# Taking the low part of every third feed-forward weight piece from an accumulating DMA instead of VectorE

## The chip, the cores and the metric

The kernel runs on one core of a Trainium2 chip. The metric is device time in microseconds (us), from a run without a profile; next to it stands one profiled execution, whose trace is read here. A core has five engines with a queue each: TensorE (PE; its weight loads are PEld), VectorE (DVE), ScalarE (ACT), GpSimd (POOL) and SyncE (SP). DMAs are issued from SP, ACT or POOL and run on the core's 16 DMA engines.

## The reference, cut to what matters

Two transformer-like blocks follow each other on 256 tokens of width 2048: first a block of gated linear recurrences, then one of windowed attention and gated linear attention, with a feed forward at its end. Only that end is touched:

```python
mixed = jnp.concatenate([attn_out, gla_out], axis=-1) @ w_out[l]        # (256,2048) @ (2048,2048)
x = x + mixed
h = rmsnorm(x, ffn_norm_w[l])
x = x + (jax.nn.silu(h @ w_gate[l]) * (h @ w_up[l])) @ w_down[l]        # hidden width 5632
return rmsnorm(x, final_norm_w)
```

All operands are float32.

## The kernel before

Every weight matrix is read once from DRAM and multiplied in a split form: a number is the sum of a high part (rounded to the matmul's float32r format) and a low part (what the rounding left). For each block of 128 input rows and each half of the tokens three matmuls are made: activation high by weight high (`wh`), activation high by weight low (`wl`), activation low by weight high, all into one PSUM bank. This is `products`, line 185.

The work is cut into **chunks** (a weight block of 16 or 22 row blocks by 512 columns, a few narrower) and each chunk into **pieces** of at most 1536 columns per partition: with 512 columns a piece holds 2 or 3 row blocks. A 16-block chunk has pieces of 2, 3, 3, 2, 3, 3 blocks, a 22-block chunk (the down matrix) 2, 3, 3, 3, 2, 3, 3, 3. A piece of n blocks is 6n matmuls, 12 or 18. There are 588 pieces in 98 chunks.

`run_stream` goes through the pieces in order. At piece i it issues `load(i+3)` (line 246: one DMA on SP into a `wr` buffer) and `cut(i+2)`: ScalarE casts `wr` into `wh` (line 259), VectorE subtracts `wh` from `wr` into `wl` (line 260). `wr`, `wh` and `wl` have three buffers each, so piece i takes the buffer of piece i-3, and its cast can't start before TensorE has read the last of piece i-3. Between the pieces, side generators put the other work of the block (transposes at line 203, the gate's tanh at line 182, `ff_up` at lines 1354 and 1355). The order of the instructions on each engine isn't that of the code alone: a scheduler in the framework puts them in the order in which, by its own costs, they become ready.

The feed forward has two halves of 2816 hidden columns. In each half come six gate chunks alternating with six up chunks (five of 512 columns and one of 256), then four down chunks. Before it stand the four chunks of the output projection (`mix_out`).

Of the kernel before, what the change touches and what calls it, by code (L numbers as in the profile page):

```python
# [11 lines left out]
F32 = mybir.dt.float32  # L12
F32R = mybir.dt.float32r
AF = mybir.ActivationFunctionType
ALU = mybir.AluOpType
# [4 lines left out]
P = 128  # L20
# [69 lines left out]
class Chunk:  # L90


    def __init__(self, src, width, nk, opnd, done, k0=0, kind="tok", tag="mm"):
        self.src, self.width, self.nk, self.opnd, self.done, self.k0 = src, width, nk, opnd, done, k0

        self.kind, self.tag = kind, tag
        self.per = max(1, min(nk, WN // width))
        self.po = None


class Opnd:
# [22 lines left out]
def kernel(ctx, tc, a, out, dbg=None):  # L124
    nc = tc.nc
    PE, V, A, G, SP = nc.tensor, nc.vector, nc.scalar, nc.gpsimd, nc.sync
# [14 lines left out]
    def nm(s):  # L141
        uid[0] += 1
        return f"{s}{uid[0]}"
# [16 lines left out]
    def v3(t, b):  # L160
        return t.rearrange("p (a b) -> p a b", b=b)
# [19 lines left out]
    def act(o, x, f, **kw):  # L181
        return A.activation(out=o, in_=x, func=f, **kw)  # L182
# [36 lines left out]
    chunks = []  # L219
# [31 lines left out]
    def cut(i):  # L251
        if i >= len(pieces) or i in split:
            return
        ch, k, n = pieces[i]
        w = raw.pop(i)
        sz = n * ch.width
        h = wp.tile([P, WN], F32R, tag="wh", name=nm("wh"), bufs=3)
        l = wp.tile([P, WN], F32R, tag="wl", name=nm("wl"), bufs=3)
        A.copy(out=h[:, :sz], in_=w[:, :sz])  # L259
        V.tensor_tensor(out=l[:, :sz], in0=w[:, :sz], in1=h[:, :sz].bitcast(F32), op=ALU.subtract)  # L260
        split[i] = (v3(h[:, :sz], ch.width), v3(l[:, :sz], ch.width))

    sides = deque()
# [1217 lines left out]
    for hf in range(2):  # L1481
        off = 0
        while off < HALF:
            w = min(512, HALF - off)
            c0 = hf * HALF + off
            add(Chunk([wg[:, c0:c0 + w]], w, 16, op3, lambda po, c0=c0, w=w: ff_gate(po, c0, w)))
            add(Chunk([wu[:, c0:c0 + w]], w, 16, op3, lambda po, c0=c0, hf=hf, w=w: ff_up(po, c0, w, hf, c0 // P)))
            off += w
        for n in range(4):
            add(Chunk([wd[:, n * 512:(n + 1) * 512]], 512, HALF // P, opf[hf],  # L1490
                      lambda po, n=n, hf=hf: ff_down(po, n, hf), k0=hf * HALF // P))
    startup()
    run_stream()

# [22 lines left out]
```

## Time and profile before

| | us |
|---|---|
| median of the two timed runs (2348.87 and 2351.42) | 2350.14 |
| the profiled execution's own time | 2350.77 |
| its span, first to last instruction | 2349.0 |
| TensorE busy in the span | 2330.5 |
| VectorE busy | 1384.8 |
| ScalarE busy | 1062.6 |
| GpSimd busy | 91.1 |

The profiled execution lies 0.6 us above the median, and 1.8 us of it are outside the span. Busy times are sums over the span; those of TensorE overlap the pipelined ends of its matmuls. The feed forward and the two chunks ahead of it take about the last 690 us.

### The profile page before, as it was taken

Reading aid. Unit: us, or ns where it says so; the run is one execution under the profiler, and the core shown is the slowest. Engines: PE = TensorE matmul, PEld = TensorE weight load, DVE = VectorE, ACT = ScalarE, POOL = GpSimd, SP = SyncE. Lnnn points to the kernel's source line nnn. Section 1 sums busy time; section 2 is a strip of 40 time slices with the busy share of each in tenths; the row PEclk is TensorE's granted clock in tenths of the full one; section 3 lists DMA queues with packets and bytes.
Section 4 is the critical chain, followed back from the end, with each engine's and each line's share of the span. In section 5 each row is a group of like instructions: output and inputs, shape, how many; then the busy total and the mean of one; then the engine's idle time right before and its main releaser. Section 6 shows DMA issues by size and latency. Waiting matters only on the chain.

```text
span 2349.0 us, 28535 instructions
## 1 busy us (share of the span) xinstructions
PE 2330.5 (99%) x11392; PEld 1930.0 (82%) x11392; DVE 1384.8 (59%) x1689; ACT 1062.6 (45%) x1240; POOL 91.1 (4%) x122
## 2 busy tenths in 40 slices
PE   8999999999999999999999999999999999999998
PEld 6888888888888888888887877888888888888886
DVE  6778677686576555455555566655545544555554
ACT  5554444544454444444444465444444333434443
POOL 0101001000000000000000000000000000000000
PEclk9999999999999999999999999999999999999999
DMA  6656545665555556566565544556655555665554
GB/s 207 188 177 202 180 142 157 188 196 188 169 159 163 180 188 210 184 200 210 180 219 179 157 141 130 166 180 201 188 192 186 191 191 187 192 194 187 188 197 152
DMA packets 226340, 427.89 MB, mean 182 GB/s; under 512 B 17256, under 2 KB 25872, under 8 KB 226208
## 3 DMA queue, kind: packets, MB, share of 16 engines
q1 hardware_dynamic: 220288, 411.07, 54.7%
q0 software_dynamic: 5056, 13.70, 2.1%
q8 instruction: 89, 1.46, 0.2%
q10 hardware_dynamic: 864, 1.31, 0.2%
q14 instruction: 43, 0.35, 0.0%
HBM read 422.31 MB, written 3.73 MB: 181 GB/s over the span
## 4 chain that ended last, share of the span: by engine, by line
PE 98%; DMA 1%; ACT 0%; issue 0%; DVE 0%; SPq 0%; POOLq 0%; POOL 0%; ACTq 0%; DVEq 0%
PE mm L185 91%; PE sp L185 4%; PE sp L203 3%; PE sp L699 1%; PE sp L1129 0%; DMA wr<-in_w_in_dram 0%; DMA pg<-in_x_dram 0%; ACT pg L182 0%; DVE wl L260 0%; ACT wh L259 0%; ACT hl L182 0%; SPq L246 0%; DVE pg L179 0%; ACT hp L182 0%; POOLq L1513 0%
## 5 line engine op out<-in xcount | busy, mean ns | idle before, releaser
L185 PE MATMUL mm<-wh,hl 128*128 128x512 f32 (+1 forms) x4864 | 1500.1, 387 | 1.6 <-ACT wh L259 1.6
L260 DVE TENSOR_TENSOR wl<-wr,wh 128x1536 fp32r<-128x1536 f32 (+3 forms) x588 | 919.3, 1567 | 751.6 <-ACT wh L259 750.7
L259 ACT CAST wh<-wr 128x1536 fp32r<-128x1536 f32 (+3 forms) x588 | 780.4, 1328 | 994.7 <-PE mm L185 943.1
L185 PEld LDWEIGHTS mm<-wh,hl 128*128 128x128 f32 x4864 | 904.7, 188 | 183.2 <-issue 4.9
L185 PE MATMUL mm<-wl,hl 128*128 128x512 f32 (+1 forms) x2432 | 941.9, 387 | 1.3 <-DVE wl L260 1.3
L185 PEld LDWEIGHTS mm<-wl,hl 128*128 128x128 f32 x2432 | 458.0, 188 | 89.7 <-DVE wl L260 1.9
L185 PE MATMUL mm<-wh,pg 128*128 128x512 f32 x1472 | 456.0, 390 | 0.0
L185 PEld LDWEIGHTS mm<-wh,pg 128*128 128x128 f32 x1472 | 276.2, 188 | 57.0
L185 PE MATMUL mm<-wl,pg 128*128 128x512 f32 x736 | 287.4, 390 | 0.0
L185 PEld LDWEIGHTS mm<-wl,pg 128*128 128x128 f32 x736 | 138.2, 188 | 29.2 <-DVE wl L260 0.9
L203 PE MATMUL sp<-con,pg 128*128 128x128 f32 x555 | 88.3, 275 | 4.1 <-DMA pg<-in_consts_dram 4.0
L203 PEld LDWEIGHTS sp<-con,pg 128*128 128x128 f32 x555 | 68.9, 141 | 21.0 <-issue 6.0
L179 DVE SCALAR_TENSOR_TENSOR pg<-cv,vt,pg 128x255 f32<-128x255 f32 (+2 forms) x144 | 61.4, 478 | 7.6 <-ACT pg L182 7.5
L185 PE MATMUL sp<-pg,pg 128*128 128x128 f32 (+3 forms) x320 | 50.7, 316 | 0.0
L179 DVE SCALAR_TENSOR_TENSOR pg<-pg,mm 128x512 f32<-128x512 f32 (+1 forms) x60 | 39.9, 665 | 16.5 <-ACT pg L182 14.8
L185 PEld LDWEIGHTS sp<-pg,pg 128*128 128x128 f32 (+1 forms) x320 | 43.0, 190 | 6.1 <-issue 2.5
L182 ACT ACTIVATE pg<-mm,rh 128x512 f32<-128x512 f32 x40 | 27.2, 687 | 33.8 <-PE mm L185 33.8
L182 ACT ACTIVATE pg<-pg 128x512 f32<-128x512 f32 (+2 forms) x54 | 35.3, 676 | 12.1 <-DVE pg L792 4.9
L182 ACT ACTIVATE pg<-mm,rstd 128x512 f32<-128x512 f32 x36 | 24.4, 687 | 32.2 <-PE mm L185 32.2
L182 ACT ACTIVATE pg<-sp,vt 128x256 fp32r<-128x256 f32 (+1 forms) x48 | 21.5, 471 | 25.7 <-PE sp L203 14.4
L179 DVE SCALAR_TENSOR_TENSOR hl<-sp,vt,hl 128x256 fp32r<-128x256 f32 x48 | 21.7, 479 | 14.0 <-ACT hl L182 13.9
L182 ACT ACTIVATE hl<-sp,vt 128x256 fp32r<-128x256 f32 x48 | 21.2, 478 | 16.1 <-PE sp L203 10.9
(245 smaller groups left out, 871.2 us busy)
## 6 DMA issues: line engine op xcount, KB each, us to landing
wr<-in_w_in_dram SPq DMA_DIRECT2D x208, 768.0 KB, 4.5
wr<-in_w_in_dram SPq DMA_DIRECT2D x104, 512.0 KB, 4.6
wr<-in_w_out_dram SPq DMA_DIRECT2D x48, 768.0 KB, 4.5
wr<-in_w_down_dram SPq DMA_DIRECT2D x48, 768.0 KB, 4.4
wr<-in_w_gate_dram SPq DMA_DIRECT2D x42, 768.0 KB, 4.4
wr<-in_w_up_dram SPq DMA_DIRECT2D x42, 768.0 KB, 4.4
wr<-in_w_out_dram SPq DMA_DIRECT2D x24, 512.0 KB, 5.1
wr<-in_w_gate_dram SPq DMA_DIRECT2D x20, 512.0 KB, 4.8
```

Of the source, the lines that this page charges most:

```text
L179: return V.scalar_tensor_tensor(out=o, in0=x, scalar=s, in1=y, op0=op0, op1=op1)
L182: return A.activation(out=o, in_=x, func=f, **kw)
L185: PE.matmul(o, l, r, start=start, stop=stop)
L203: PE.transpose(o, x, ident[:n, :n])
L259: A.copy(out=h[:, :sz], in_=w[:, :sz])
L260: V.tensor_tensor(out=l[:, :sz], in0=w[:, :sz], in1=h[:, :sz].bitcast(F32), op=ALU.subtract)
L699: PE.matmul(o, l, r_, start=True, stop=True, tile_position=(row, col))
```

## The change

A chunk gets a flag `acc`, set on the last 34 chunks: the second half of the output projection and the whole feed forward. In them, each piece whose number is a multiple of three gets its low part in another way. ScalarE writes minus the high part into `wl` (an activation with scale -1, whose output is rounded to float32r as the cast's is); then GpSimd issues a DMA that reads the same weights from DRAM a second time and adds them onto `wl`. The subtract on VectorE is left out for these pieces. There are 69 of them: 60 with 3 blocks of 512 columns, 5 with 2 blocks, 4 in the chunks of 256 columns. As three buffers go round, they are always the same buffer of `wl`.

```diff
@@ class Chunk
+        self.acc = False
@@ cut
         A.copy(out=h[:, :sz], in_=w[:, :sz])
-        V.tensor_tensor(out=l[:, :sz], in0=w[:, :sz], in1=h[:, :sz].bitcast(F32), op=ALU.subtract)
+        if ch.acc and i % 3 == 0:
+
+            act(l[:, :sz], w[:, :sz], AF.Copy, scale=-1.0)
+            G.dma_start(out=v3(l[:, :sz], ch.width), accum_op=ALU.add,
+                        in_=ch.src[0][(ch.k0 + k) * P:(ch.k0 + k + n) * P, :].rearrange("(k p) n -> p k n", p=P))
+        else:
+            V.tensor_tensor(out=l[:, :sz], in0=w[:, :sz], in1=h[:, :sz].bitcast(F32), op=ALU.subtract)
@@ the end of the list of chunks
+    for ch in chunks[-34:]:
+        ch.acc = True
     startup()
     run_stream()
```

Line numbers of the changed kernel are one higher up to line 260 and seven higher behind it; the new activation goes through the helper at line 183, the new DMA is line 264.

Three places show the new order. On ScalarE, in an up chunk of the first half, `wl2055` is the low part of a piece of the new kind, `wh2054` its high part, `wr2050` its raw weights, and `pg2056` the gate's tanh. Before:

```order
L259 CAST wh2051_12884<-wr2047_12864 128x1024 [waits DMAHW6_49,DVE_49,PE_49]
L259 CAST wh2054_12908<-wr2050_12882 128x1536 [waits DMAHW7_49,DVE_49,PE_49]
L182 ACTIVATE pg2056_12930<-mm2035_12786,r3h_117 128x512 [waits PE_49]
L182 ACTIVATE pg2056_12930<-mm2036_12787,r3h_117 128x512 [waits PE_49]
L259 CAST wh2058_12937<-wr2053_12906 128x1536 [waits DMAHW0_49,DVE_49]
```

After:

```order
L260 CAST wh2051_12898<-wr2047_12878 128x1024 [waits DMAHW6_49,DVE_49,PE_49]
L183 ACTIVATE wl2055_12923<-wr2050_12896 128x1536 [waits DMASW3_49,DMAHW7_49,PE_49,Activation_49]
L260 CAST wh2054_12922<-wr2050_12896 128x1536 [waits PE_49,Activation_49]
L183 ACTIVATE pg2056_12945<-mm2035_12799,r3h_117 128x512 [waits PE_49]
L183 ACTIVATE pg2056_12945<-mm2036_12800,r3h_117 128x512 [waits PE_49]
L260 CAST wh2058_12952<-wr2053_12920 128x1536 [waits DMAHW0_49,DVE_49]
```

The minus-high activation stands ahead of the cast of its own piece, and both ahead of the tanh, where one cast stood.

On TensorE, in the first gate chunk of the second half, `wh2313` and `wl2314` belong to a piece of the new kind, and `wh2316`, `wl2317` to the 2-block piece behind it. Before:

```order
L185 MATMUL mm2304_14659<-wh2313_14723,hl1878_11738 128x512 [waits Activation_49]
L185 MATMUL mm2305_14660<-wh2313_14723,hl1878_11738 128x512
L185 MATMUL mm2304_14659<-wl2314_14724,hl1878_11738 128x512 [waits DVE_49]
L185 MATMUL mm2304_14659<-wh2313_14723,hl1878_11738 128x512 x2
L185 MATMUL mm2304_14659<-wl2314_14724,hl1878_11738 128x512
```

After:

```order
L186 MATMUL mm2304_14697<-wh2313_14761,hl1878_11738 128x512 [waits Activation_49]
L186 MATMUL mm2305_14698<-wh2313_14761,hl1878_11738 128x512
L186 MATMUL mm2325_14838<-wh2316_14780,hl1878_11738 128x512 [waits Activation_49]
L186 MATMUL mm2326_14839<-wh2316_14780,hl1878_11738 128x512
L186 MATMUL mm2325_14838<-wl2317_14781,hl1878_11738 128x512 [waits DVE_49]
L186 MATMUL mm2325_14838<-wh2316_14780,hl1878_11738 128x512 x2
...
L186 MATMUL mm2304_14697<-wl2314_14762,hl1878_11738 128x512 [waits DMASW4_49]
```

All 12 matmuls of the 2-block piece now stand between the first two matmuls of the piece and its first `wl` matmul, which waits for the accumulating DMA. The order has this form at 13 of the 69 pieces, nearly all in the second half; at the piece of the new kind that comes next, only one 3-block piece is then left between it and the last piece of its kind.

On TensorE, in a gate chunk of the first half, `wl2076` is of the new kind, and `sp2084`, `sp2091` are transposes of the up chunk before. Before:

```order
L185 MATMUL mm2081_13078<-wh2075_13047,hl1878_11738 128x512
L185 MATMUL mm2080_13077<-wl2076_13048,hl1878_11738 128x512 [waits DVE_49]
L185 MATMUL mm2080_13077<-wh2075_13047,hl1878_11738 128x512 x2
L185 MATMUL mm2080_13077<-wl2076_13048,hl1878_11738 128x512
L185 MATMUL mm2080_13077<-wh2075_13047,hl1878_11738 128x512 x2
L203 MATMUL sp2084_13093<-con_84,pg2056_12930 128x128 [waits DVE_49]
```

After:

```order
L186 MATMUL mm2081_13095<-wh2075_13063,hl1878_11738 128x512
L204 MATMUL sp2084_13110<-con_84,pg2056_12945 128x128 [waits DVE_49]
L204 MATMUL sp2091_13157<-con_84,pg2056_12945 128x128 [waits PE_49]
L204 MATMUL sp2084_13110<-con_84,pg2056_12945 128x128 [waits DVE_49]
L204 MATMUL sp2084_13110<-con_84,pg2056_12945 128x128 x2
L204 MATMUL sp2091_13157<-con_84,pg2056_12945 128x128 x3
L186 MATMUL mm2080_13094<-wl2076_13064,hl1878_11738 128x512 [waits DMASW6_49]
```

Eight transposes have moved ahead of the first `wl` matmul; this is so at 7 pieces.

## Rows read from the trace of the kernel before

**Rows 1.** The page, its parts 1, 4 and 5: TensorE, the chain, two groups.

```profile
PE 2330.5 (99%) x11392; PEld 1930.0 (82%) x11392; DVE 1384.8 (59%) x1689; ACT 1062.6 (45%) x1240; POOL 91.1 (4%) x122
...
PE 98%; DMA 1%; ACT 0%; issue 0%; DVE 0%; SPq 0%; POOLq 0%; POOL 0%; ACTq 0%; DVEq 0%
...
L185 PE MATMUL mm<-wh,hl 128*128 128x512 f32 (+1 forms) x4864 | 1500.1, 387 | 1.6 <-ACT wh L259 1.6
...
L185 PE MATMUL mm<-wl,hl 128*128 128x512 f32 (+1 forms) x2432 | 941.9, 387 | 1.3 <-DVE wl L260 1.3
```

**Rows 2.** Two stretches of the feed forward: busy us by engine, clock, DMA share, GB/s.

```profile
1700.00:1836.00 136.00, 136.00 (x637) 113.43 (x636) 69.64 (x56) 56.62 (x50) 0.00 (x0) 1.00 0.59 188
...
1960.00:2200.00 240.00, 240.00 (x1094) 199.23 (x1093) 122.47 (x96) 98.38 (x85) 0.00 (x0) 1.00 0.60 190
```

**Rows 3.** Who waited for whom from 1640 us on: total, times, longest.

```profile
ACT wh L259 <- PE mm L185: 358.9, 169, 3.0
DVE wl L260 <- ACT wh L259: 316.4, 174, 3.3
```

**Rows 4.** Timeline of ScalarE: start, duration, what, idle before it.

```profile
1774.71 1.48 ACT L259 CAST wh<-wr 128x1536 fp32r<-128x1536 f32 x1 [2.60 <-PE mm L185]
1777.43 1.05 ACT L259 CAST wh<-wr 128x1024 fp32r<-128x1024 f32 x1 [1.24 <-PE mm L185]
1781.51 1.48 ACT L259 CAST wh<-wr 128x1536 fp32r<-128x1536 f32 x1 [3.02 <-PE mm L185]
...
1834.13 1.27 ACT L259 CAST wh<-wr 128x1280 fp32r<-128x1280 f32 x1
...
1838.15 1.26 ACT L259 CAST wh<-wr 128x1280 fp32r<-128x1280 f32 x1 [1.21 <-PE mm L185]
```

**Rows 5.** Timeline of TensorE around the same piece.

```profile
1774.06 0.39 PE L185 MATMUL mm<-wl,hl 128*128 128x512 f32 x1
...
1781.77 0.39 PE L185 MATMUL mm<-wl,hl 128*128 128x512 f32 x1
...
1782.45 0.39 PE L185 MATMUL mm<-wl,hl 128*128 128x512 f32 x1
```

**Rows 6.** Timeline of VectorE, the subtract of the same piece.

```profile
1776.23 1.76 DVE L260 TENSOR_TENSOR wl<-wr,wh 128x1536 fp32r<-128x1536 f32 x1 [2.32 <-ACT wh L259]
```

**Rows 7.** Groups by shape, whole span: count, busy us, mean ns, idle before.

```profile
L259 ACT CAST wh<-wr 128x1536 fp32r<-128x1536 f32 x388 | 574.2, 1480 | 773.5 <-PE mm L185 737.9 <-issue 22.3 <-DMA wr<-in_w_in_dram 11.9
...
L259 ACT CAST wh<-wr 128x1024 fp32r<-128x1024 f32 x184 | 193.6, 1052 | 209.7 <-PE mm L185 194.7 <-issue 9.1 <-ACT wh L259 3.5
...
L182 ACT ACTIVATE pg<-pg 128x1024 f32<-128x1024 f32 x14 | 14.8, 1058 | 5.0 <-DVE pg L792 4.9
```

**Rows 8.** Line 986, plain loads of 512 KB issued from GpSimd.

```profile
L986 POOL DMA_DIRECT2D pg<-in_x_dram x4: 727/744/755, 855.0 to 1097.7; - x4
...
DMA to landing us min/median/max: 4.1/4.4/5.2
```

**Rows 9.** Tile wr from 1700 us on: weight loads issued from SP.

```profile
L246 SPq DMA_DIRECT2D wr<-in_w_down_dram x64: 367/368/368, 1836.9 to 2319.0; - x64
...
DMA to landing us min/median/max: 3.6/4.4/6.4
```

**Rows 10.** Line 1374, loads of one DRAM row to all partitions, from GpSimd.

```profile
L1374 POOL DMA_DIRECT2D hp<-in_final_norm_w_dram x4: 536/539/604, 1611.9 to 2284.6; - x4
...
DMA to landing us min/median/max: 5.3/6.2/7.1
```

**Rows 11.** DMA from 1900 to 1922 us in 40 slices: busy tenths, GB/s.

```profile
DMA  9960001499985999526999300037973001399964
GB/s 287 335 250 34 0 0 37 93 335 376 410 205 93 354 384 410 194 63 156 372 357 354 127 0 0 0 48 197 324 268 115 0 0 11 82 313 384 398 268 104
```

**Rows 12.** Two stretches at the start, columns as in rows 2.

```profile
0.00:10.00 10.00, 5.98 (x32) 6.01 (x33) 0.76 (x3) 4.88 (x13) 1.79 (x7) 1.00 0.77 249
...
20.00:30.00 10.00, 7.07 (x31) 4.85 (x32) 5.73 (x13) 5.95 (x11) 0.00 (x0) 1.00 0.70 228
```

## The prediction

> **What bounds the kernel now.** I read the page first: TensorE is busy 99% of the span and makes 98% of the chain that ended last; before its `wh` and `wl` matmuls it idled 1.6 and 1.3 us in the whole run [rows 1]. The stretches of the feed forward say the same of the stage that is changed: TensorE 136.00 of 136.00 and 240.00 of 240.00 us, VectorE about half, ScalarE about four tenths, the DMA engines 0.59 and 0.60 of their time [rows 2]. The waits there show who follows whom: ScalarE's cast waits for TensorE (358.9 us in 169 waits), VectorE's subtract for the cast (316.4 us), and TensorE for neither [rows 3]. So VectorE's 69 subtracts, 1.76 us each [rows 6], lie beside other work. Taking them away can give back at most the 2.9 us of idling in rows 1. What is left to ask is whether the new path brings `wl` before TensorE wants it.
>
> **The window of a piece.** Rows 4 to 6 show one ordinary 3-block piece that would be of the new kind. The last `wl` matmul of the piece three before it, whose buffer it takes, starts at 1774.06 and ends at 1774.45. The cast starts at 1774.71; the 2-block piece is through 2.72 us later and the 3-block piece 4.08 us after that (next casts at 1777.43 and 1781.51), and the first `wl` matmul of the piece itself starts at 1781.77 [rows 4, 5]. A matmul takes a place of 0.227 us (three between 1781.77 and 1782.45). A handover costs 0.04 us: the cast ends at 1776.19, the subtract starts at 1776.23 [rows 4, 6].
>
> In the changed kernel ScalarE's minus-high activation stands first. It waits only for that last `wl` matmul, so it starts at 1774.49. Its length: an activation of 1024 columns takes 1058 ns where a cast takes 1052, so one of 1536 takes what the cast takes, 1.48 us [rows 7]. It ends at 1775.97, GpSimd's DMA starts at 1776.01, and TensorE wants the sum at 1781.77. The window is **5.76 us** from issue to landing. What is longer is a stall of TensorE, once per piece, and nothing gives it back: the next piece of the kind starts its own window when this one has been read.
>
> The order of the changed kernel gives each of the 69 pieces its window, in matmuls of 0.227 us and transposes of 0.11 us between the same two events:
> - 24 pieces have 5.76 us, one 6.03.
> - 8 have seven or eight transposes (or three) moved ahead: seven 6.64, one 6.85.
> - 12 (and one of the narrow chunks) have the whole next piece moved ahead of their first `wl` matmul: 8.5 to 9.6 us.
> - 13 pay for that: the piece moved ahead is missing from their own window, since it was read before their buffer came free. Five have 3.04 us, four 3.92 (with transposes), three 3.27, one 3.39.
> - 2 have two 3-block pieces before them, 7.12; the five 2-block pieces too, and their activation is shorter: 7.55.
> - The other four sit at or in the narrow chunks with 30 matmuls in 4.02 us (casts at 1834.13 and 1838.15, rows 4): 7.4, 7.6, 7.7 and 9.2. This counts 24+1+8+12+13+2+5+4 = 69.
>
> **What the DMA takes.** No row shows an accumulating DMA. The nearest is the plain load that GpSimd issues from DRAM in 2 KB rows beside the weight stream: 512 KB land in 4.4 us (4.1 to 5.2), of which the issue is 0.74 [rows 8]. The third block is 256 KB more; at the 384 to 410 GB/s of the fullest slices [rows 11] that is 0.66 us, so 5.1 us for a plain load of 768 KB. The weight loads of SP show less growth: 4.4 us in the median for pieces of both sizes [rows 9]. So the low end is 4.4 us, if the add costs nothing. The add has to read the 768 KB that stand in `wl` as well: 786 thousand bytes at 400 GB/s are 1.97 us more, 7.0 us. The engines are 0.6 busy with weight loads [rows 2]; if the extra read only gets the free 0.4 of them, it takes 4.7 us, and the load lands after 9.8 us. That is the high end; loads from one DRAM row on the same queue, 6.2 us for 256 KB [rows 10], show that 4.4 is no ceiling there. I take **7.5 us**, nearer to the undisturbed value: rows 11 show several slices in a row with the engines idle between two weight loads, and the accumulating DMA is issued about 1.5 us ahead of the next weight load (that one waits for the cast behind the activation to free `wr`).
>
> The Trainium skill ("Collectives: The Full Stack", section "The bandwidth ceiling: the fold count and why AG ≠ RS ≠ AR") says that an add in the DMA path emits two reads per chunk on one ring and so runs at half the rate of a copy; no run here shows it. With one read the landing would be 5.1 us and the sum 22; by that rule it is 7.0 us on undisturbed engines, and the same windows give 80. The skill's fit for a DMA from GpSimd ("DMA: Bandwidth & Descriptors", section "Anatomy of one DMA — SWDGE (gpsimd) path"), 2.0 us plus bytes over 436 GB/s, speaks for the shorter time: 3.8 us for 768 KB, 5.6 us with the bytes counted twice, and the sum would be about 30 us. The trace disagrees at 512 KB: the fit gives 3.2 us and rows 8 show 4.4.
>
> **The sum at 7.5 us.** 24 x 1.74 = 41.8; 1.5; 7 x 0.86 + 0.65 = 6.7; the short windows 5 x 4.46 + 4 x 3.58 + 3 x 4.23 + 4.11 = 53.4; 2 x 0.38 = 0.8; the narrow ones 0.1; the 12 long windows 0; the 2-block pieces 0 (a third fewer bytes land 1.3 us sooner, 6.2 of 7.55). Together **104 us**. On the profiled execution's own 2350.8 us that is 2455; on the median, 0.6 us below it, as good as the same.
>
> The other edits cost nothing where they are covered. The 69 extra activations (102 us) fall on ScalarE, which is idle for more than half of the stage. Queued behind each is the cast of its own piece, which ends 2.8 us after the buffer came free and is wanted 3.9 us after it even in the short windows; without that cover it would add its 1.48 us. The tanh behind both is up to 1.5 us later; its PSUM banks are wanted a chunk of some 22 us later. On GpSimd each DMA waits for ScalarE with the loads at line 1374 queued behind it; the last of these is wanted after the last down piece. The transposes moved ahead wait for VectorE's product, which loses 1.76 us of subtract from its queue. The weight loads have 4.4 us to land and a window of about 7.6 (from 3.3 us after one cast until the cast 10.9 us later), so 3 us of delay are covered. TensorE's clock was granted in full (1.00) while it was busy only 5.98 and 7.07 of 10 us [rows 12], so I charge no clock for stalls of 2 to 4 us.
>
> **The rivals.** (1) *The add is free or nearly so.* Then it lands in 4.4 to 5.1 us, inside every window but the 13 short ones: 5 x 2.06 + 4 x 1.18 + 3 x 1.83 + 1.71 = 22 us at 5.1, 13 us at 4.4, so 2364 to 2373: not slower by 2%. It decides up to a landing of 6.2 us, where the sum reaches 47 us. For it: rows 9, where more bytes cost no time; against it: the bytes must be read from somewhere. (2) *The add works row by row, reading and writing each with a latency of its own.* A landing of 12 us gives 390 us by the same windows, 2740. Nothing in the profile speaks for it but that nothing shows the operation. (3) *VectorE was holding TensorE after all*, and the change gains: rows 1 allow 2.9 us, so 2348; 2% would need 47. (4) *The change doesn't do what it says*, the order hiding the new wait: it does so at 13 pieces only, and takes it from the 13 next ones; between them a pair has the same 11.5 us as two ordinary pieces, so this is in the sum already.
>
> **How the numbers follow.** A landing between 6.2 and 9.8 us, my forecast: 0.61. Rival 1: 0.26. Rival 2 and all landings above 9.8 us: 0.12. A gain: 0.01. The landing of 9.8 us gives 239 us, 2590; 4.4 us gives 2364. Leaving out rival 2's 0.12 at the top and some 0.05 below, the range is 2364 to 2590. Slower by over 2% (about what a measurement of this kernel can tell from no change) is 0.61 + 0.12 = 0.73, within 2% 0.26, faster 0.01.
>
> **What would show it.** In the changed profile TensorE should wait for a DMA into `wl` at line 186 in some 45 to 50 of the 69 pieces, 100 us in total, the longest over 4 us at pieces that follow one with the 2-block piece moved ahead; the landing of line 264 in the median should read 7 to 8 us; the GpSimd issue under 1.3 us; ScalarE's new activation 1.48 us; the DMA share of the stage 0.7 or more. A landing under 6 us or over 10 makes the prediction wrong, as would waits of TensorE for a cast or for `wr`, which I count at nothing.

## The result, and the profile after

| | before | after |
|---|---|---|
| median of the timed runs (2 each) | 2350.14 | 2636.92 (2634.54 and 2639.3) |
| span of the profiled execution | 2349.0 | 2632.7 |
| TensorE busy in the span | 2330.5 | 2422.5 |

The change makes the kernel slower: the ratio is 1.1219, with a 95% interval of 1.1192 to 1.1246. The forecast was 2455 in a range of 2364 to 2590, so the direction was right and the loss is some 2.7 times the one forecast, beyond the range.

The page of the changed kernel shows where to look: its parts 1, 3, 4 and 5.

```profile
PE 2422.5 (92%) x11392; PEld 1982.5 (75%) x11392; DVE 1268.6 (48%) x1620; ACT 1151.6 (44%) x1309; POOL 180.0 (7%) x191
...
q1 hardware_dynamic: 220288, 411.07, 48.0%
q0 software_dynamic: 33296, 66.40, 14.2%
...
PE mm L186 5%; DMA wl<-in_w_down_dram 3%; DMA wl<-in_w_up_dram 3%; DMA wl<-in_w_gate_dram 2%; DMA wr<-in_w_up_dram 2%; DMA wr<-in_w_gate_dram 1%; ACT wl L183 1%; ACT wh L260 1%; DMA wr<-in_w_down_dram 0%; ACT pg L183 0%; DVE wl L267 0%; ACTq L183 0%; DVE pg L180 0%; ACT hp L183 0%; POOLq L1522 0%
...
L186 PE MATMUL mm<-wl,hl 128*128 128x512 f32 (+1 forms) x2432 | 969.7, 399 | 133.8 <-DMA wl<-in_w_up_dram 67.9
...
L186 PE MATMUL mm<-wl,pg 128*128 128x512 f32 x736 | 299.4, 407 | 59.9 <-DMA wl<-in_w_down_dram 44.1
L183 ACT ACTIVATE wl<-wr 128x1536 fp32r<-128x1536 f32 (+1 forms) x69 | 100.2, 1452 | 421.4 <-PE mm L186 378.7
```

TensorE's share fell from 99% to 92%, and the idle time before its `wl` matmuls rose from 1.3 us [rows 1] to 133.8 in the gate and up chunks and 59.9 in the others, nearly all of it behind a DMA into `wl`. But two things don't fit a plain wait. TensorE is also *busy* 92 us longer with the same 11392 matmuls. And waits of 134 + 60 us don't add up to the 283.7 by which the span grew.

The waits from 1600 us on (total, times, longest), and below them line 264, the accumulating DMAs:

```profile
PE mm L186 <- DMA wl<-in_w_up_dram: 67.9, 22, 4.6
PE mm L186 <- DMA wl<-in_w_gate_dram: 64.6, 22, 4.8
PE mm L186 <- DMA wl<-in_w_down_dram: 44.1, 20, 4.1
...
ACT wl L183 <- DMA wr<-in_w_up_dram: 17.5, 5, 4.2
```

```profile
L264 POOL DMA_DIRECT2D wl<-in_w_up_dram x22: 1267/1277/1502, 1658.5 to 2459.9; - x22
...
DMA to landing us min/median/max: 7.3/9.5/11.2
```

Four more, 15.8 us, stand behind the adds of the output projection, two of them ahead of 1600 us. So TensorE waits at 68 of the 69 pieces; 66 of these waits are over 0.3 us, 192.0 us together. The issue on GpSimd takes 1.28 us and the landing 9.5 us in the median, where 7.5 was taken.

One ordinary piece, an up piece of the first half. ScalarE and GpSimd first, then TensorE (start, duration, what, idle before):

```profile
1792.40 1.49 ACT L183 ACTIVATE wl<-wr 128x1536 fp32r<-128x1536 f32 x1 [9.34 <-PE mm L186]
```

```profile
1794.19 1.28 POOL L264 DMA_DIRECT2D wl<-in_w_up_dram  x1 [16.11 <-ACT wl L183]
```

```profile
1798.96 0.84 PE L186 MATMUL mm<-wh,hl 128*128 128x512 f32 x3
1803.66 0.80 PE L186 MATMUL mm<-wl,hl 128*128 128x512 f32 x1 [3.87 <-DMA wl<-in_w_up_dram]
1804.25 1.06 PE L186 MATMUL mm<-wh,hl 128*128 128x512 f32 x2
1805.11 0.63 PE L186 MATMUL mm<-wl,hl 128*128 128x512 f32 x1
...
1808.52 0.43 PE L186 MATMUL mm<-wl,hl 128*128 128x512 f32 x1
1808.79 0.62 PE L186 MATMUL mm<-wh,hl 128*128 128x512 f32 x2
```

The DMA is issued at 1794.19 and TensorE goes on at 1803.66, 9.47 us later, after 3.87 us of idling; the window of 5.76 us leaves 3.71. (The activation ends at 1793.89, so the handover to GpSimd took 0.30 us, where the prediction had 0.04.) What no term of the forecast has stands behind the wait: ten matmuls from 1804.25 to 1808.52 start 0.427 us apart, not 0.227, and from 1808.79 on the old pace is back. The stretches of the same piece show why (busy us of the engines, then granted clock, DMA share, GB/s):

```profile
1803.66:1808.50 4.84, 4.84 (x11) 3.84 (x12) 0.00 (x0) 0.00 (x0) 0.00 (x0) 0.50 0.61 235
1808.50:1815.00 6.50, 6.50 (x30) 5.37 (x29) 0.00 (x0) 3.87 (x3) 1.28 (x1) 0.99 0.21 24
```

The granted clock is 0.50 (1.2 of 2.4 GHz) behind the wait and 0.99 after it. The Trainium skill ("TensorE: Matmul & The Clock Gate", section "Wait — 56ns, not 53.3ns?") has 426.7 ns between matmuls of 512 columns at 1.2 GHz; the trace's 0.427 us agrees.

Over the whole stage:

```profile
1625.00:1996.00 371.00, 289.12 (x1194) 233.88 (x1193) 90.32 (x86) 132.97 (x119) 29.42 (x24) 0.89 0.64 172
1996.00:2604.00 608.00, 515.58 (x2202) 416.50 (x2201) 167.90 (x139) 242.94 (x205) 55.48 (x46) 0.94 0.76 200
```

The clock's mean was 1.00 there before [rows 2]; it is 0.89 in the gate and up chunks of the first half, and 0.94 from there to the last add.

So the books nearly close. The 66 waits are 192.0 us. Each costs 0.16 more, since the profile counts idling from the end of the last matmul (0.39 us long), not from its place of 0.227: 10.6. Over the timeline from 1540 to 2625 us I count 343 matmuls that follow the one before by 0.33 to 0.445 us, none in the kernel before; beyond 0.2275 us each they take 63.5. The first matmul behind a wait holds its place for 0.59 us in 18 cases and for some 0.34 in nearly all the others, also behind short waits that no slow matmul follows: 12 us, of which the clock has 18 x 0.25 = 4.5. Together 278 of the 283.7 us; the rest was not placed.

Of the 38 waits of over 3 us, 34 have slow matmuls behind them, 5 to 11 each; of the 20 under 2 us, none has.

### The profile page after: what moved, and what is told of

It reads as the page before. It is cut to its first block, busy times and chain, and to the rows that moved or that the text cites. A ratio compares the mean times of both kernels' runs of the same rounds, so it can differ in the third digit from the quotient of the medians.

```text
span 2632.7 us, 28740 instructions
## 1 busy us (share of the span) xinstructions
PE 2422.5 (92%) x11392; PEld 1982.5 (75%) x11392; DVE 1268.6 (48%) x1620; ACT 1151.6 (44%) x1309; POOL 180.0 (7%) x191
## 3 DMA queue, kind: packets, MB, share of 16 engines
q0 software_dynamic: 33296, 66.40, 14.2%
## 5 line engine op out<-in xcount | busy, mean ns | idle before, releaser
L186 PE MATMUL mm<-wh,hl 128*128 128x512 f32 (+1 forms) x4864 | 1535.1, 395 | 1.0 <-ACT wh L260 1.0
L267 DVE TENSOR_TENSOR wl<-wr,wh 128x1536 fp32r<-128x1536 f32 (+3 forms) x519 | 801.2, 1547 | 907.7 <-ACT wh L260 906.6
L186 PE MATMUL mm<-wl,hl 128*128 128x512 f32 (+1 forms) x2432 | 969.7, 399 | 133.8 <-DMA wl<-in_w_up_dram 67.9
L186 PEld LDWEIGHTS mm<-wh,hl 128*128 128x128 f32 x4864 | 930.7, 194 | 190.8 <-issue 4.9
L186 PEld LDWEIGHTS mm<-wl,hl 128*128 128x128 f32 x2432 | 473.3, 195 | 241.7 <-DMA wl<-in_w_up_dram 76.7
L186 PE MATMUL mm<-wl,pg 128*128 128x512 f32 x736 | 299.4, 407 | 59.9 <-DMA wl<-in_w_down_dram 44.1
L186 PEld LDWEIGHTS mm<-wh,pg 128*128 128x128 f32 x1472 | 285.5, 194 | 60.1
L183 ACT ACTIVATE wl<-wr 128x1536 fp32r<-128x1536 f32 (+1 forms) x69 | 100.2, 1452 | 421.4 <-PE mm L186 378.7
L171 DVE TENSOR_TENSOR pg<-pg,mm 128x512 f32<-128x512 f32 (+1 forms) x24 | 15.4, 643 | 94.5 <-PE mm L186 94.5
L264 POOL DMA_DIRECT2D wl<-in_w_up_dram x22 | 28.5, 1297 | 320.4 <-ACT wl L183 302.0
L264 POOL DMA_DIRECT2D wl<-in_w_gate_dram x22 | 28.5, 1298 | 304.3 <-ACT wl L183 304.3
L264 POOL DMA_DIRECT2D wl<-in_w_down_dram x21 | 26.4, 1258 | 280.2 <-ACT wl L183 280.2
```

Source lines behind the costliest of these rows:

```text
L171: V.tensor_tensor(out=o, in0=x, in1=y, op=ALU.mult)
L186: PE.matmul(o, l, r, start=start, stop=stop)
L264: G.dma_start(out=v3(l[:, :sz], ch.width), accum_op=ALU.add, in_=ch.src[0][(ch.k0 + k) * P:(ch.k0 + k + n) * P, :].rearrange("(k p) n -> p ...
```

## The experiments

Each differs from the changed kernel (or, where said, from it with a part undone) by the lines shown. Runs with one time have no interval; the kernel before lay between 2348 and 2354 us beside all of them.

**1. The same DMA without the add.**

```diff
-            G.dma_start(out=v3(l[:, :sz], ch.width), accum_op=ALU.add,
+            G.dma_start(out=v3(l[:, :sz], ch.width),
```

> The GpSimd DMA copies the weights into wl without adding (so wl holds the whole weight, not its low part); the minus-high activation in front of it stays. Theory A (each row of the add costs the DMA engines two reads, 184 ns in place of 92, and that makes the landing 9.5 us late, the stalls, and the half clock behind them): the copy lands in 5 to 6 us, q0's packets take about 92 ns a row, TensorE stalls only in the 13 short windows, 20 to 45 us in all, the clock stays near 1.00, time 2370 to 2400. Theory B (GpSimd's issue of 1.28 us and the sharing with the weight stream make the landing late, the add itself is cheap): landing 8 to 9 us, stalls over 130 us, time above 2530.

Measured: 2376.61 us (one run). Line 264 in its profile, then the waits from 1600 us:

```profile
L264 POOL DMA_DIRECT2D wl<-in_w_up_dram x22: 775/775/865, 1629.5 to 2229.9; - x22
...
DMA to landing us min/median/max: 4.8/5.1/8.8
```

```profile
PE mm L186 <- DMA wl<-in_w_up_dram: 8.8, 7, 1.9
PE mm L186 <- DMA wl<-in_w_down_dram: 8.2, 6, 2.3
```

Everything else of the change is still there, and 260 of the 287 us are gone. The activation, the wait, the second transfer of the weights and the new order cost 26 us in all; the adding costs the rest. The copy lands in 5.1 us in the median, to the digit what the prediction worked out for a plain load of 768 KB, but 24 of the 69 took over 6 us, up to 8.8. The waits left, 17 with 19.8 us in all, come near the 22 us that it listed under rival 1, but by luck: at nine of its short windows, from 2013 to 2200 us, they are 6.3 us together (it had 5 x 2.06 + 4 x 1.18 = 15), and the rest stands mostly at ordinary pieces with a late copy.

**2. Copy and add alone.** Eight extra DMAs at the end of the kernel, when no weight load runs, copy and add in turn:

```diff
+    t = wp.tile([P, WN], F32R, tag="wl", name=nm("wl"), bufs=3)
+    for r in range(4):
+        blk = wg[r * 384:(r + 1) * 384, 0:512].rearrange("(k p) n -> p k n", p=P)
+        G.dma_start(out=v3(t, 512), in_=blk)
+        G.dma_start(out=v3(t, 512), accum_op=ALU.add, in_=blk)
```

> The changed kernel with eight DMAs from GpSimd added behind its last work, one after the other on one tile: copy and add of the same 768 KB in turn, with no weight stream beside them. Theory A: a copy lands in 4.2 to 5 us, an add 1.8 to 2.8 us later than a copy. Theory B: both within 0.7 us of each other. The difference between the add here and the 9.5 us in the stream is the price of sharing: I expect 2 to 3 us.

Measured: 2675.77 us (one run; the time itself says only that the tail is longer). The copies are line 1506, the adds line 1507:

```profile
L1506 POOL DMA_DIRECT2D wl<-in_w_gate_dram x4: 792/798/799, 2618.4 to 2659.3; - x4
...
DMA to landing us min/median/max: 4.8/4.9/7.0
```

```profile
L1507 POOL DMA_DIRECT2D wl<-in_w_gate_dram x4: 1270/1282/1318, 2623.7 to 2664.5; - x4
...
DMA to landing us min/median/max: 7.3/7.3/7.5
```

Undisturbed, 768 KB are added in 7.3 us and copied in 4.9: the add costs 2.4 us more, 0.5 of it in the issue. The remaining 2.2 us of the 9.5 in the stream come from something else there.

**3. One buffer more for these pieces.** `wl` of the new kind gets two buffers of its own, the others share two; two other buffers had to be given up for the room.

```diff
-PGB = 23
+PGB = 22
...
-MB = 4
+MB = 3
...
-        l = wp.tile([P, WN], F32R, tag="wl", name=nm("wl"), bufs=3)
+        l = wp.tile([P, WN], F32R, tag="wl" if i % 3 else "wa", name=nm("wl"), bufs=2)
```

> The pieces of the new kind get two wl buffers of their own, the others two (one buffer more in all; one page and one small buffer fewer), so the minus-high activation waits for the weight load alone and no more for TensorE. Theory A (the window against the landing, and the clock as its consequence): the window grows by about 3 us, stalls fall under 1 us a piece and the half clock is gone, time 2350 to 2400, within 2% of the kernel before. Theory C (the extra DMA traffic itself slows the weight stream, so that TensorE waits for wr and wh instead): time stays above 2450, with waits for wr.

Measured: 2492.44 us (4 runs), ratio 1.0604 [1.0584, 1.0625]. What ScalarE waited for ahead of its activation, from 1600 us:

```profile
ACT wl L183 <- DMA wr<-in_w_down_dram: 141.2, 21, 10.6
ACT wl L183 <- DMA wr<-in_w_gate_dram: 128.5, 22, 9.1
ACT wl L183 <- DMA wr<-in_w_up_dram: 113.1, 22, 8.6
```

Half the loss comes back, not all of it. With the buffer free early, the activation waits for its raw weights instead: the weight loads, 4.4 us in the median before [rows 9], land after 7.3 us (from 3.6 up to 11.4) beside the adds. TensorE's waits for the adds fell from 192 to 54 us, but now it waits 26 us for VectorE's subtracts and 8 for casts, which it did not in the changed kernel; the other pieces have two `wl` buffers here, not three, so the run does not price the longer lead alone. A buffer lengthens the window only up to the landing of the raw weights; for more, they would have to come earlier too. Theory A's 2350 to 2400 fell; the time and the late `wr` are what theory C had.

**4. The waits filled.** Ten dummy matmuls, into a bank that nobody reads, stand between the first `wh` and the first `wl` matmul of every such piece, so that TensorE is busy while it would have waited. Nearly no piece is moved ahead in this order.

```diff
+                if keep and j == 0 and o == 0:
+                    b = bank()
+                    for _ in range(keep):
+                        mm(b[:, :ch.width], hi, wh)
...
+            keep = 10 if ch.acc and i % 3 == 0 else 0
```

> Ten more matmuls of 512 columns into an unused PSUM bank (2.27 us) stand between the first wh matmul and the first wl matmul of each piece of the new kind; their result is read by nobody. The order has nearly no piece moved ahead any more. Theory A: the pieces wait as long as before, so the sum of idling and of these matmuls is 200 to 230 us, but the idle stretch is at most some 2 us and the granted clock stays 1.00: time 2540 to 2590, about 50 to 95 us faster than the changed kernel although it computes more. Theory D (no cost hangs on the clock; the 90 us beyond the idling have another cause): time 2630 or more.

Measured: 2632.29 us (one run). The theory's 2540 to 2590 was missed, and the time by itself is theory D's; what speaks for the clock is found by stretches. From the first gate add to the first down add (the gate and up chunks of the first half) it took 339.7 us against 370.8 in the changed kernel, but the same chunks of the second half took 340.8 against 315.2. The half clock is all but gone (stretches of the first half's gate and up chunks, and of the rest):

```profile
1620.00:1959.00 339.00, 303.15 (x1407) 247.45 (x1406) 91.34 (x86) 132.55 (x118) 29.12 (x23) 0.99 0.70 188
1959.00:2602.00 643.00, 584.59 (x2626) 477.50 (x2625) 168.81 (x139) 243.95 (x206) 55.48 (x45) 0.98 0.71 190
```

In the first of them TensorE's waits for `wl` fell from 81.9 to 35.8 us, the dummies take 22 x 10 x 0.227 = 50, and it is 31 us shorter all the same. By the difference that leaves some 35 us to the clock; the slow-paced matmuls counted there give 28 (from 32.8 to 4.5 us). In the second half the pieces that the order had moved ahead were no longer moved; the dummies stand there beside waits that were short before, which lost more than the clock gave.

**5. The dummies in the first half alone.** As in 4, with `keep` only in the first 18 of the 34 chunks, up to the first half's down chunks, so that the second half has the changed kernel's order.

```diff
+            keep = 10 if ch.acc == 2 and i % 3 == 0 else 0
...
+    for ch in chunks[-34:-16]:
+        ch.acc = 2
```

> The ten extra matmuls stand only in the first 18 of the 34 chunks (the half whose order has no piece moved ahead), the second half is as in the changed kernel. In the run with them everywhere the stretch from the first gate issue to the first down issue took 339.7 us against 370.8, with as long a wait. If that is the clock, the time is 2590 to 2615 (some 30 us under the changed kernel) with the granted clock near 1.00 in that half and as low as before in the other; if it isn't the clock, 2632 or more.

Measured: 2624.47 us (4 runs, 2616.1 to 2631.57), ratio 1.1153 [1.1128, 1.1178]: 12 us faster than the changed kernel, not the 22 to 47 of the theory. In the profiled run the gate and up chunks of the first half took 343.2 us, 27.6 less than in the changed kernel. Up to their end (from 1540 us on) the slow-paced matmuls went from 193 to 50, and the time that they take beyond the usual pace from 36.4 to 7.8 us: 28.6, about the gain. What it lost again is found by chunks: the first half's down chunks took 171.4 us against 160.1, since they have the dummies too and several waits there were only 1 us long; the gate and up chunks of the second half took 325.3 against 315.2, with the changed kernel's order, and from their start to the end of the kernel 28.4 us against 17.6 are slow-paced matmuls. So the half clock does not fall alike in two kernels with the same order and much the same waits (51.5 and 47.5 us, 21 each).

**6. Other pieces.** The new kind is taken at remainder 2 instead of 0. In the first half's gate and up chunks these are the 2-block pieces, with a window of 7.55 us; in the second half's they are 3-block pieces with 5.76 us, and none is moved ahead.

```diff
-        if ch.acc and i % 3 == 0:
+        if ch.acc and i % 3 == 2:
```

> The pieces whose number leaves the remainder 2 take the new path, not 0 (70 pieces). In the first half these are the 2-block pieces, with two 3-block pieces before them: a window of 7.55 us and 512 KB to add; from the second half on they are 3-block pieces with the window of 5.76 us. Theory A (window against landing, and the clock behind long stalls): in the first half 512 KB land in about 8.4 us, so under 1 us of stall a piece and no half clock; from the first gate issue to the first down issue 250 to 285 us, where the changed kernel takes 371; the second half is as slow as there. Time 2520 to 2570. Theory F (each added DMA costs about the same, whatever its window and size): the first half stays above 340 us, time 2600 or more.

Measured: 2594.65 us (one run). The gate and up chunks of the first half took 285.5 us, at the upper edge of what the window theory gave and 85 under the changed kernel; the clock was 0.96 there, not 0.89. From there to the last add it took 678.2 (608.0 in the changed kernel), and the theory's total of 2520 to 2570 was missed:

```profile
1607.00:1893.00 286.00, 261.53 (x1180) 213.02 (x1179) 100.70 (x86) 126.05 (x120) 27.89 (x24) 0.96 0.79 206
1893.00:2571.00 678.00, 544.11 (x2265) 438.09 (x2264) 171.85 (x141) 247.57 (x209) 56.83 (x46) 0.91 0.68 182
```

The window does set the wait: the adds cost 85 us less where it is 1.8 us longer and a third fewer bytes land. Of the rest, the gate and up chunks of the second half took 371.2 us: with 3-block pieces, a window of 5.76 and nothing moved ahead, what the changed kernel takes in its first half (370.9). In its own second half the changed kernel takes 315.2; so by this comparison the order that moves the 2-block pieces ahead is worth 56 us there.

**7. A light weight stream.** In the last 34 chunks SyncE loads only the first row block of each piece, and the casts read it again for the others (the weights are wrong there).

```diff
-            SP.dma_start(out=wv[:, :, c:c + cw_],
-                         in_=src[(ch.k0 + k) * P:(ch.k0 + k + n) * P, :].rearrange("(k p) n -> p k n", p=P))
+            m = 1 if ch.acc else n
+            SP.dma_start(out=wv[:, :m, c:c + cw_],
+                         in_=src[(ch.k0 + k) * P:(ch.k0 + k + m) * P, :].rearrange("(k p) n -> p k n", p=P))
```

> SP loads only the first row block of each piece of the last 34 chunks, and the casts read that block repeatedly (so the weights used are wrong for the other blocks); everything else is as in the changed kernel. The weight stream falls to about three eighths. Theory A: the add alone takes 7.3 us, and what is beyond that in the stream, 2.2 us, is sharing with the weight loads: landing 7.3 to 8.0 us, idling 90 to 130 us, clock loss 10 to 40 us, time 2450 to 2510. Theory G (the landing of 9.5 us comes from something else, such as the waits and traffic of the other engines): landing stays at 9 us or more, time above 2590.

Measured: 2531.77 us (one run). Landing 8.3 us, between the two theories; so a run with less still was made.

**8. Hardly any weight stream.** SyncE loads 64 columns of one row block per piece, 32 KB; the rest as in 7.

```diff
+            if ch.acc:
+                SP.dma_start(out=w[:, :64], in_=src[(ch.k0 + k) * P:(ch.k0 + k + 1) * P, :64])
...
+        w3 = mid(w[:, :64], sz // 64) if ch.acc else v3(w[:, :sz], ch.width)
```

> In the last 34 chunks SyncE loads only 64 columns of the first row block of every piece (32 KB instead of 512 or 768 KB), and the casts, activations and subtracts read these columns over and over (the weights there are wrong; every instruction of TensorE and the accumulating DMAs are as in the changed kernel). Theory A (an undisturbed add lands 1.95 us after a copy, 7.3 us, and all that is above it in the stream is the sharing with the weight loads): landing 7.1 to 7.6 us in the median, waits of TensorE near 95 us by the windows, 2440 to 2480 us in all. Rival H (something else holds the add, the traffic of the engines into the same memory or the length of the queue): landing 8 us or more, as with a third of the weight bytes, and over 2500 us.

Measured: 2465.56 us (4 runs), ratio 1.0481 [1.0463, 1.0498]. Line 270 is the add here:

```profile
DMA to landing us min/median/max: 6.1/7.6/9.4
```

That is 7.6 us against 7.3 alone, and rival H's 8 us or more is out. Landings of 9.5, 8.3 and 7.6 us go with 768, 256 and 32 KB of weight load for each 3-block piece: nearly all of the 2.2 us comes from the weight loads that run beside the add. It is also the forecast's own case: an add of 7.5 us was to cost 104 us, and this kernel, with 7.6, loses 114. That the two are so near is in part luck: at nine of the short windows, from 2083 to 2277 us, TensorE waits 6.4 us together where the forecast had 5 x 4.46 + 4 x 3.58 = 37, and 22 us are slow-paced matmuls, which it had at nothing.

**9. The add in three.** One accumulating DMA for each row block, so that TensorE can begin with the first.

```diff
-            G.dma_start(out=v3(l[:, :sz], ch.width), accum_op=ALU.add,
-                        in_=ch.src[0][(ch.k0 + k) * P:(ch.k0 + k + n) * P, :].rearrange("(k p) n -> p k n", p=P))
+            for q in range(n):
+                G.dma_start(out=l[:, q * ch.width:(q + 1) * ch.width], accum_op=ALU.add,
+                            in_=ch.src[0][(ch.k0 + k + q) * P:(ch.k0 + k + q + 1) * P, :])
```

> The add of a piece is issued as one DMA for each row block, so the first wl matmul waits for 256 KB and not for 768 KB. Theory A: the first block lands after 5.5 to 7 us, the last one at 9.5 to 11; the last wl block of the first token half is wanted 1.4 us after the first, so the loss is 2 to 3 us a piece in place of 4, and broken into shorter waits that keep the clock: time 2480 to 2560. Theory H (three issues on GpSimd and more descriptors cost as much as they save): time 2600 to 2660.

Measured: 2456.66 us (one run), better than the theory's lower edge. In a piece like the one shown above, TensorE waits 1.16 us instead of 3.87 (GpSimd, then TensorE):

```profile
1790.52 2.68 POOL L265 DMA_DIRECT2D wl<-in_w_up_dram  x3 [10.23 <-ACT wl L183]
```

```profile
1798.39 0.50 PE L186 MATMUL mm<-wl,hl 128*128 128x512 f32 x1 [1.16 <-DMA wl<-in_w_up_dram]
```

The waits over 0.3 us are many (69) and short (73 us together, the longest 3.5), and the clock over 1600 to 2440 us was 1.00. It is the fastest of these versions that keep the adds and the weights, and still 106 us behind the kernel before.

**10. The activation alone.** It is kept; the DMA is left out and VectorE subtracts as before.

```diff
         if ch.acc and i % 3 == 0:
             act(l[:, :sz], w[:, :sz], AF.Copy, scale=-1.0)
-            G.dma_start(out=v3(l[:, :sz], ch.width), accum_op=ALU.add, ...
-        else:
+        if True:
             V.tensor_tensor(out=l[:, :sz], in0=w[:, :sz], in1=h[:, :sz].bitcast(F32), op=ALU.subtract)
```

> Minus the high part is written as in the changed kernel, the DMA is left out, and VectorE subtracts for every piece as before (it overwrites what the activation wrote, so nothing is left out of the result). Theory A (the 69 activations on ScalarE lie beside other work): 2350 to 2356 us, TensorE's waits for wl and wh below 8 us in the stage. Rival: if the activation ahead of the cast is a part of the loss, it takes up to 69 x 1.48 = 102 us more, and TensorE waits for casts at line 186.

Measured: 2350.7 us (10 runs), ratio 0.9999 [0.9989, 1.0008]. The 100 us of extra work on ScalarE cost nothing.

**11. Late low parts without a DMA.** VectorE makes the same subtract six times over; there is neither the activation nor the DMA.

```diff
-            act(l[:, :sz], w[:, :sz], AF.Copy, scale=-1.0)
-            G.dma_start(out=v3(l[:, :sz], ch.width), accum_op=ALU.add, ...
+            for _ in range(6):
+                V.tensor_tensor(out=l[:, :sz], in0=w[:, :sz], in1=h[:, :sz].bitcast(F32), op=ALU.subtract)
```

> No activation and no DMA: for the 69 pieces VectorE makes the same subtract six times in a row (the result is the same), which brings wl 8.8 us later than before. From the window of 7.3 us after the buffer comes free, 1.75 of it to the end of the cast and six times 1.76 for the subtracts, TensorE should wait 4 to 5 us in an ordinary piece of the first half, as it did behind the accumulating DMA, but with no extra traffic. Theory A (the half clock follows a long wait of TensorE, whatever it waited for): in the first half more than 20 us of half clock in 10 or more intervals, and the run's time lies 30 us or more above 2350 plus the sum of the waits. Rival B (the half clock has to do with the accumulating DMA itself): no more than two intervals of half clock in the feed forward, and the time is 2350 plus the sum of the waits, within 15 us.

Measured: 2842.21 us (4 runs), ratio 1.2088 [1.2068, 1.2108]. Where TensorE waited for the six, at every second piece of the first half's gate and up chunks, the waits were longer than meant, 6.8 us in the mean, because VectorE's other work stands between the six. A wait, and the stretches around it:

```profile
1805.78 0.79 PE L186 MATMUL mm<-wl,hl 128*128 128x512 f32 x1 [6.59 <-DVE wl L264]
1806.37 1.05 PE L186 MATMUL mm<-wh,hl 128*128 128x512 f32 x2
```

```profile
1805.78:1808.93 3.15, 3.15 (x8) 2.47 (x9) 0.00 (x0) 0.00 (x0) 0.00 (x0) 0.50 0.61 166
1808.93:1812.00 3.07, 3.07 (x15) 2.53 (x14) 0.00 (x0) 0.73 (x1) 0.00 (x0) 0.99 0.03 6
...
1612.00:2033.00 421.00, 300.54 (x1150) 233.87 (x1151) 311.49 (x220) 103.20 (x94) 1.80 (x3) 0.85 0.36 111
```

The half clock is there without one accumulating DMA and at a DMA share of 0.36. All of TensorE's waits from 1540 us on come to 357 us, and the span grew by 492. Rival B, that the adds themselves lower the clock, is out: the clock follows TensorE's idling, whatever it waits for.

## Why the prediction was right in direction and wrong in size

**What bounds the kernel, and what the change can give: right.** VectorE's 69 subtracts lay beside other work; the profile after has 116 us less work on VectorE and nothing gained by it.

**The ordinary window: right but for 0.3 us.** The add shown was issued at 1794.19, and TensorE went on 9.47 us later after 3.87 of idling, 4.03 with the 0.16: it wanted the sum 5.44 us after the issue, not 5.76. The difference is the handover from ScalarE to GpSimd, 0.30 us where the prediction took the 0.04 that rows 4 and 6 show between ScalarE and VectorE. Experiment 6 moves the window, and the wait follows.

**The landing: mis-sized, the main failed step.** The sum was made of 5.1 us for the copy, 1.97 for the second read and about 0.5 for sharing the engines: 7.5. The first two were about right: 5.1 us in experiment 1, and in experiment 2 the add takes 2.4 us longer than the copy, 0.5 of it issue (1.28 us; "under 1.3" was right as well). The rule cited from the Trainium skill ("Collectives: The Full Stack", section "The bandwidth ceiling: the fold count and why AG ≠ RS ≠ AR"), stated there for the reduce step of a collective, two reads for an add, agrees with the traces in direction: a 2 KB row of the accumulating DMA holds a DMA engine for 184 ns, of the copy in experiment 1 for 109 (the share of queue q0, 14.2% here, 10.2% there and 2.1% before, each of 16 engines' span; the difference, over 28,240 added packets). The skill's other figure, the fit for a DMA from GpSimd ("DMA: Bandwidth & Descriptors", section "Anatomy of one DMA — SWDGE (gpsimd) path"), gave 3.8 us for the copy, and the trace disagrees again, with 4.9 alone. The third was wrong: sharing costs 2.2 us, not 0.5, and 9.5 is nearly the 9.8 that stood as the high end. My reason for the low value was that the add starts ahead of the next weight load and that the engines idle between two loads. The fill of the DMA engines from 1790 to 1812 us (slices of 0.55 us; busy tenths, GB/s) shows what that is worth:

```profile
DMA  0000000000097699999999999999980000000010
GB/s 0 0 0 0 0 0 0 0 0 0 0 67 86 89 209 261 246 238 261 261 261 253 268 339 395 417 413 406 413 331 30 0 0 0 0 0 0 0 30 0
```

The add has the engines to itself for two slices; then the weight load, issued only 1.1 us behind it (at 1795.29), runs beside it to the end, at 238 to 268 GB/s together where the loads alone reach 400 and more. From 1798.2 to 1802.2 us the trace counts 248 rows of the add, 177 ns each on an engine, and 250 of the load, 100 ns each: row for row, so while a load is there the add gets less of the engines than it would alone. Idle engines on the average did not help, because both start in the same few microseconds and the idle time lies afterwards.

At 9.5 us the prediction's own windows give 24 x 3.74 = 90, 3.5, 7 x 2.86 + 2.65 = 23, the short windows 79, 5 for the two of 7.12, and some 14 for the long, narrow and 2-block ones: 215 us. The waits measured 192, or 202.6 with the 0.16 each. So by the prediction's own sum a landing of 9.5 gives 2566 us, still inside its range; what took the time out of it stands under the clock, below.

**The short windows: wrong, too dear by half.** They were to wait longest. They did not: the nine pieces from 2190 to 2417 us that follow a moved-ahead one waited 1.7 to 3.9 us, 2.9 in the mean, where the windows give 6. From the issue of the add until TensorE wanted it they had 6.2 to 8.0 us, not 3.0 to 3.9. The longest waits (up to 4.8) stand at other pieces. The mistake was in the buffers. At one of them, ScalarE's activation for the piece behind, and the first and the last (the sixth) `wl` matmul of the piece ahead, which is of the new kind too:

```profile
2178.80 1.49 ACT L183 ACTIVATE wl<-wr 128x1536 fp32r<-128x1536 f32 x1 [3.26 <-DMA wr<-in_w_up_dram]
```

```profile
2178.47 0.50 PE L186 MATMUL mm<-wl,hl 128*128 128x512 f32 x1 [1.28 <-DMA wl<-in_w_gate_dram]
2178.81 0.62 PE L186 MATMUL mm<-wh,hl 128*128 128x512 f32 x2
...
2181.78 0.39 PE L186 MATMUL mm<-wl,hl 128*128 128x512 f32 x1
```

The activation writes its `wl` from 2178.80 on, while TensorE reads the `wl` of the last piece of the kind until 2182. So it has another buffer, and "always the same buffer" does not hold. That the buffer of the piece moved ahead, which is free first, is the one handed on fits all of this, but no trace names the buffer. What held the activation back was its raw weights (3.26 us behind `wr`), for which I had charged nothing; such waits come to 38 us in 12 pieces, part of the 2.9 us above. The pieces with the long window waited 1.0 to 2.4 us. Rival 4 was so half right: the order hides part of the new wait, and does not take it back at the next piece (56 us, experiment 6).

**TensorE's clock: wrong, the second failed step, and the one that took the time out of the range.** It was charged at nothing, because stretches with TensorE busy 5.98 and 7.07 of 10 us had the full clock [rows 12]. Neither stretch bears that out. In the second the idling comes in pieces, the longest 1.06 us. In the first it is one wait of 4.02 us ahead of the first matmul, as in this timeline of the kernel before, from 0 to 10 us:

```profile
4.02 0.88 PE L203 MATMUL sp<-con,pg 128*128 128x128 f32 x3 [4.02 <-DMA pg<-in_consts_dram]
4.68 3.19 PE L203 MATMUL sp<-con 128*128 128x128 f32 x14
7.67 2.52 PE L203 MATMUL sp<-con,pg 128*128 128x128 f32 x15
```

The 14 transposes from 4.68 to 7.67 start 0.213 us apart, and so do those up to 9 us; from there on it is 0.109. That is half the pace for 5 us, behind an idle time of 4 us: what the changed kernel shows behind 39 of its waits was there to be read. The 1.00 of that row is no sign against it, since the trace has no record of the clock ahead of 9.1 us and counts that as full. Behind waits of 3 to 5 us in the changed kernel the matmuls run at 0.427 us for up to 5 us. That is 63.5 us in counted matmuls and 4.5 of the 12 in the first ones, some 68 of the 284; without them, by this count, the time would be 2569 us, inside the range. Experiment 11 shows that the cause is the wait, experiments 4 and 5 that filling the wait brings it back (28 us in each, counted in slow matmuls of the first half), experiment 9 that short waits hardly cause it.

**The rest.** The activation took 1.49 us, as taken [rows 7], and cost nothing (experiment 10). The DMA share was to be 0.7 or more: 0.64 and 0.76. Waits were to come in 45 to 50 pieces, a number that went with 7.5 us; at 9.5 it was 68. Rival 1 (the add is free) lost by 4.4 us of landing, rival 2 (row by row, 12 us) by 2.5: 2740 would have been nearer in time, but by a landing that did not happen. In the terms of the forecast, 104 us became about 200 by the landing (less what the short windows gave back), some 68 more came from the clock and 8 from the slower start of the first matmul behind each wait; some 6 were not placed.

## What to carry to other kernels

Moving work from an engine that has spare time to a DMA trades a hidden cost for a latency, and the latency has to fit into the window that the buffers leave: work that out first, and price the DMA beside the transfers that start with it, not by the engines' mean share. If a wait of a few microseconds on TensorE comes out, add the slow matmuls behind it, here 2 us for a wait of 4; and check a granted clock of 1.00 against the pace of the matmuls in the same stretch. Where the data can be consumed in parts, land it in parts: three smaller adds cost 106 us here where one cost 287.

## What the runs showed of the hardware

- An accumulating DMA of 768 KB from GpSimd takes 1.28 us to issue and lands 7.3 us after its start alone, 7.6 beside a stream of 32 KB loads, 8.3 with 256 KB, 9.5 with 768 KB. The plain copy: 0.78 us and 4.9 alone, 5.1 in the stream. The copy's median hardly minds the stream, though 24 of the 69 copies in it took over 6 us; the add's does.
- The adds slow the loads beside them: down weight loads of 768 KB landed after 6.2 us, gate and up loads after 6.3 and 7.4, where the median was 4.4 [rows 9].
- TensorE's granted clock fell to 0.50 with a wait of 3.87 us and came back 4.9 us after its end; it fell with a wait of 6.59 us for VectorE too (experiment 11). In the kernel before, the transposes behind the wait of 4.02 us at its start ran at half their later pace for 5 us. In experiment 8 the matmuls behind a wait of 2.26 us ran at the slow pace for 3.5 us.
- Open: what decides after which of two like waits the clock falls. Experiment 5 shows 28.4 us of slow-paced matmuls from the second half's gate chunks on, where the changed kernel, with the same order, shows 17.6.
